# A causal convolution with matrix taps: the first four outputs as direct products, then 21 blocks of twelve

## The chip, the cores and the metric

The kernel runs on one core of a Trainium2 chip. The metric is device time in microseconds (us) of one execution, from one launch; lower is better. The kernel before has three timed runs, with a median of 758.33 us. A core's engines are named as in the profile: PE is TensorE (matmul), DVE VectorE, ACT ScalarE, POOL GpSimd, SP SyncE, which here only issues transfers.

## The reference, cut to what matters

```python
# x: (8, 4096, 512) f32, kernel: (8, 512, 512) f32
out = zeros_like(x)
for k in range(8):
    shifted = x moved by k rows along S, zeros in front
    out += matmul(shifted, kernel[k])
```

So each output row is the sum of eight products of a 512-vector of x, from 0 to 7 rows back, with a 512x512 matrix ("tap" 0 to 7).

## The kernel before, in words

The 8 x 4096 rows are cut into 128 runs of 256 consecutive rows. Run number is the partition, so "output t" (0 to 255) means row t of all 128 runs at once, and `x[t]` is a 128x512 tile. x is kept transposed in bfloat16, four 128x128 pieces to a tile, in the ring `XR` of 20 places (`place(t)`). A product (`product`, line 116) is one such tile times one 512x512 matrix: four matmuls of 128x128 by 128x512, summed in PSUM.

Eight products for each output would be the direct way. The kernel instead takes twelve outputs, t to t+11, as a block of four nodes, each a four-tap filter that gives four rows. The taps are split in two halves, `H1` (taps 4 to 7) and `H0` (taps 0 to 3); the nodes work with `H1`, `H0`, their difference `MI` (H0 - H1) and their sum `PL` (H0 + H1), each on sums or differences of x, and results are combined to rows. Tap `7 - (4a + 2b + c)` lies in `W[H1 or H0, b, c]`, with b and c each LO, HI; MID stands for a difference of LO and HI. Within a node the same trick is used again: a full node takes 9 products (`a1`, `a0`, `u` on the sums A and Z; `v0`, `v1` on S; four `l` on F), and a leaf node 11 (`a1`, `a0`, `u`, then eight on S, without F, `v` and `d`). H0 is a leaf in every block, so a block has 9 + 9 + 9 + 11 = 38 products.

DVE makes the inputs (`zsum`: Z from XR, then A, S, F), the weight sums (`wsum`, `plus`), the differences within PSUM (`node_d`) and, at the end of a node (`node_e`), combines outputs. ACT seeds PSUM (`node_seed`), copies the quad (`node_a1`, `node_dts`) and copies results out. POOL issues the loads from DRAM (they cast f32 to bf16), and transfers that add one SBUF tile to another (`add_h0`, line 328). SP issues the stores and the transposing transfers from a bf16 copy of x in DRAM into XR. Each of these queues works in the order of the program text.

The first 16 outputs of each run (`HEAD`) are made by six nodes of another form, n0 to n5 (lines 303 to 308): n0 as 16 direct products on summed inputs, n1 to n3 as leaves (`LEAF`), n4 and n5 as full nodes; their results are kept (some in the memory of PL weights, `held`) and combined by `node_y`. In this stage the order of the instructions is written out by hand (lines 331 to 561): loads, PE transposes of the first rows, weight sums as taps arrive, fills (matmuls on zeros, whose results are not used) and the six nodes. Then come 20 blocks, whose order is given by the `SLOT` table; node k runs while node k+1 is seeded and the inputs of k+2 are summed.

Memory that is used twice: early x lies in tiles that later hold weights (`xin`), and early results do too; a weight sum into such a tile waits until the last reader, a store among them, is done. PSUM has four pairs of banks; three go round over the nodes, the fourth holds the quad.

Of the kernel before, what the change touches and what calls it, by code (L numbers as in the profile page):

```python
# [14 lines left out]
def kernel(  # L15
# [210 lines left out]
    def node_y(n, b_, a):  # L226
        y = first[n.t, a, b_]
        tt(y, y, n.p[b_], ADD if a == H1 else SUB)

    def store_first(t, a, b_):  # L230
        store(t + 4 * a + 2 * b_, first[t, a, b_])

    def node_e(n, b_):
        p, t = n.p[b_], n.t + 2 * b_
        if n.k < 4:
            y = wide(held[n.k, b_]) if (n.k, b_) in held else y_tile()
            nc.scalar.copy(out=y, in_=p)
            first[n.t, n.a, b_] = y
        elif n.k < 6:
            node_y(n, b_, H1)  # L240
            node_y(n, b_, H0)
        elif n.a == PL:
# [42 lines left out]
    H, HF = XR[:, 8:16], wide(WP[:, 0:8])  # L285
    XF = XR[:, 0:8]
    xin = {(0, 0): WP[:, 12:16], (0, 4): WP[:, 16:20], (8, 0): W[PL, LO, LO], (8, 4): W[PL, HI, LO]}

    def load_xin(t, h):
        rows(xin[t, h], t + h, 4)  # L290
# [12 lines left out]
    nodes = [  # L303
        Node(0, 0, H1),
        Node(1, 8, H1, (T4[:, 0], [D42[:, 7]] + [T42[:, j] for j in range(4)])),
        Node(2, 0, H0, (D4[:, 4], [D42[:, j] for j in range(3, 8)])),
        Node(3, 8, H0, (D4[:, 4], [D42[:, j] for j in range(3, 8)])),
        Node(4, 0, MI), Node(5, 8, MI)]
    nodes += [Node(6 + 4 * k + i, HEAD + STEP * k, a) for k in range(NB)
              for i, a in enumerate((PL, MI, H1, H0))]  # L310
    n0, n1, n2, n3, n4, n5, n6, n7 = nodes[:8]
    def direct(m, t):
        n = K // 2 - 1 - m
        product(n0.p[t // 2][:, t % 2], D4[:, t - m] if t >= m else E4[:, 4 + t - m],
                W[H1, n >> 1, n & 1], m == 0)
# [16 lines left out]
    nc.vector.memset(zero, 0.0)
    for k in range(6):
        fill(pair(k % 4))
    load_xin(0, 0)
    fill(pair(2))
    make_identity(nc, ident)
    transpose_pe("x0", 2, xin[0, 0], 0, 2)
    load_xin(0, 4)
    rows(H[:, 1:4], RUN - 7, 3)  # L340
    nc.sync.dma_start(out=HF, in_=xr[:, RUN - 4:RUN, :])
    load_w(4)
    nc.scalar.copy(out=H[:, 4:6], in_=HF[:, 0:2])
    load_w(5)
    nc.scalar.copy(out=H[:, 6:8], in_=HF[:, 2:4])
    nc.scalar.copy(out=XF[:, 4:6], in_=bank["x0"])
    transpose_pe("h0", 3, H, 4, 6)
    nc.scalar.copy(out=to(XF[:, 0:2]), in_=prev(bank["h0"]))
    first_run(XF[:, 0:2])
    fill(pair(3))  # L350
    fill(pair(2))
    tt(D4[:, 0:2], XF[:, 0:2], XF[:, 4:6], ADD)
    transpose_pe("h1", 0, H, 6, 8)
    nc.scalar.copy(out=to(XF[:, 2:4]), in_=prev(bank["h1"]))
    first_run(XF[:, 2:4])
    fill(pair(3))
    fill(pair(3))
    load_xin(8, 0)
    transpose_pe("xb", 0, xin[0, 0], 2, 4)
    direct(0, 0)  # L360
    load_w(6)
    nc.vector.tensor_copy(out=XF[:, 6:8], in_=bank["xb"])
    tt(D4[:, 2:4], XF[:, 2:4], XF[:, 6:8], ADD)
    direct(0, 1)
    transpose_pe("he", 1, H, 1, 4)
    fill(pair(2))
    fill(pair(2))
    seed_plus(HI, HI)
    direct(0, 2)
    transpose_pe("x1", 2, xin[0, 4], 0, 4)  # L370
    tt(to(E4[:, 1:4]), prev(bank["he"]), to(XF[:, 1:4]), ADD)
    first_run(E4[:, 1:4])
    load_w(7)
    fill(pair(3))
    fill(pair(3))
    direct(1, 1)
    nc.vector.tensor_copy(out=X4, in_=bank["x1"])
    fill(pair(3))
    tt(D42[:, 3], D4[:, 1], D4[:, 3], ADD)
    transpose_pe("x2", 2, xin[8, 0], 0, 4)  # L380
    direct(1, 2)
    load_w(3)
    nc.scalar.copy(out=X8[:, 2:4], in_=bank["x2"][:, 2:4])
    tt(D4[:, 4:8], XF[:, 4:8], X4, ADD)
    tt(D42[:, 4:8], D4[:, 2:6], D4[:, 4:8], ADD)
    wsum(H1, MID, HI)
    wsum(H1, MID, LO)
    direct(2, 0)
    nc.scalar.copy(out=X8[:, 0:2], in_=bank["x2"][:, 0:2])
    tt(T4, X4, X8, ADD)  # L390
    direct(0, 3)
    direct(3, 1)
    nc.scalar.mul(out=W[MI, HI, LO], in_=W[H1, HI, LO], mul=-1.0)
    fill(pair(3))
    direct(3, 0)
    direct(3, 2)
    direct(2, 1)
    wsum(H1, MID, MID)
    tt(AX[1][:, 0], D4[:, 7], T4[:, 0], ADD)
    fill(pair(2))  # L400
    tt(T42[:, 2:4], T4[:, 0:2], T4[:, 2:4], ADD)
    direct(3, 3)
    load_w(1)
    wsum(H0, MID, LO)
    load_w(0)
    load_w(2)
    tt(AX[1][:, 1], T4[:, 0], T4[:, 1], ADD)
    wsum(MI, HI, HI)
    node_a1(n1)
    tt(T42[:, 0:2], D4[:, 6:8], T4[:, 0:2], ADD)  # L410
    direct(2, 2)
    direct(1, 3)
    node_a0(n1)
    node_u(n1)
    node_seed(n1, 0)
    direct(2, 3)
    direct(1, 0)
    wsum(H0, MID, HI)
    wsum(H0, MID, MID)
    load_xin(8, 4)  # L420
    load_x(16)
    node_l(n1, 0, LO)
    tt(AX[0], D4[:, 3:5], D4[:, 4:6], ADD)
    node_e(n0, 0)
    node_seed(n1, 1)
    node_l(n1, 0, HI)
    node_s(n5)
    wsum(MI, LO, HI)
    wsum(MI, MID, HI)
    nc.scalar.copy(out=D4[:, 2:4], in_=T4[:, 2:4])  # L430
    add_h0(MI, HI, LO)
    node_s(n4)
    node_l(n1, 1, HI)
    node_a1(n2)
    wsum(MI, LO, LO)
    node_e(n0, 1)
    node_a0(n2)
    node_e(n1, 0)
    transpose(12, xin[8, 4])
    wsum(MI, LO, MID)  # L440
    tt(D4[:, 4:8], X8, XR[:, 16:20], ADD)
    node_u(n2)
    node_seed(n2, 0)
    seed_plus(LO, HI)
    node_A(n4)
    node_l(n1, 1, LO)
    node_l(n2, 0, LO)
    nc.scalar.copy(out=D42[:, 3], in_=T42[:, 3])
    add_h0(PL, LO, HI)
    node_l(n2, 0, HI)  # L450
    node_seed(n2, 1)
    node_a1(n3)
    node_l(n2, 1, LO)
    tt(AX[1], D4[:, 3:5], D4[:, 4:6], ADD)
    node_u(n3)
    node_a0(n3)
    wsum(MI, MID, LO)
    behind(AX[1][:, 0])
    load_x(36)
    node_e(n1, 1)  # L460
    node_l(n2, 1, HI)
    node_e(n2, 0)
# [174 lines left out]
```

## Time and profile before

| | |
|---|---|
| runs | 757.30, 758.33, 759.14 us; median 758.33 |
| profiled execution | 759.11 us, with a span of 757.3 us from first to last instruction |
| PE busy | 733.1 us, 97% |
| DVE busy | 690.1 us, 91% |
| ACT, POOL busy | 254.9 us, 62.0 us |
| granted PE clock, mean | 0.993 of full |
| DMA | 141.51 MB, mean 187 GB/s |
| weight loads | 8 of 512 KB (as written), median 20.8 us from issue to landing |
| adding transfers, SBUF to SBUF | 5, median 6.8 us |
| stores | 124 of 512 KB from output tiles, median 7.7 us |

Of the page, the slices give the busy share of 40 equal parts of the span in tenths; the answer by stretches gives busy time and instruction count of each engine; the chain follows what ended last back from step to step. A matmul's duration overlaps the next one's, so a rate is read from starts. Line numbers are those of the kernel before.

### The profile page before, as it was taken

How to read it: one execution, taken by the hardware profiler on the slowest of the kernel's cores; microseconds unless marked ns; L12 is line 12 of the kernel's file. 1: busy time of each engine (PE TensorE's matmuls, PEld its weight loads, DVE VectorE, ACT ScalarE, POOL GpSimd, SP SyncE). 2: the span in 40 equal slices, each digit the busy share in tenths (PEclk: the TensorE clock that was granted, in tenths of full speed). 3: DMA queues.
4: the chain of work that ended last, by engine and by line, in shares of the span. 5: the costliest groups of instructions: out<-in, count | busy, mean ns of one | idle time of the engine just before them, and what ended most of it. 6: DMA issues, size and time to landing. Idle time of an engine off the chain costs nothing.

```text
span 757.3 us, 8900 instructions
## 1 busy us (share of the span) xinstructions
PE 733.1 (97%) x3352; PEld 331.8 (44%) x3420; DVE 690.1 (91%) x727; ACT 254.9 (34%) x380; POOL 62.0 (8%) x103
## 2 busy tenths in 40 slices
PE   6999689999999999999999999999999999999997
PEld 2544234444444444444444444444444444444443
DVE  1774899999999999999999999999999999999996
ACT  4264332333333233333323333332423323232331
POOL 5020201010010101101010110101011010100000
PEclk9999899999999999999999999999999999999999
DMA  9979797976959688796968869796786969775424
GB/s 206 207 140 162 195 255 173 211 200 161 245 136 237 162 195 215 149 238 148 243 160 180 241 140 236 146 238 168 185 234 136 242 145 224 184 178 169 136 84 167
DMA packets 159948, 141.51 MB, mean 187 GB/s; under 512 B 130208, under 2 KB 134304, under 8 KB 159776
## 3 DMA queue, kind: packets, MB, share of 16 engines
q1 hardware_dynamic: 145456, 99.89, 48.6%
q0 software_dynamic: 14304, 40.77, 29.6%
q8 instruction: 27, 0.44, 0.2%
q10 hardware_dynamic: 144, 0.26, 0.1%
q14 instruction: 17, 0.14, 0.1%
HBM read 77.33 MB, written 98.57 MB: 232 GB/s over the span
## 4 chain that ended last, share of the span: by engine, by line
PE 91%; DMA 4%; DVE 2%; issue 1%; ACT 0%; POOL 0%; DVEq 0%; ACTq 0%; POOLq 0%
PE pp L118 91%; DMA w<-in_kernel_dram 2%; DMA out_dram<-w 1%; DMA XR<-xd 1%; DVE y L82 1%; DVE w L82 1%; PE pp L295 0%; DVE S L82 0%; PE pp L300 0%; ACT pp L188 0%; DVE Z L82 0%; DVE F L82 0%; ACT pp L169 0%; ACT pp L190 0%; DVE pp L82 0%
## 5 line engine op out<-in xcount | busy, mean ns | idle before, releaser
L118 PE MATMUL pp<-w,S 128*128 128x512 bf16 x1114 | 261.6, 381 | 5.7 <-ACT pp L190 3.9
L118 PE MATMUL pp<-w,F 128*128 128x512 bf16 x973 | 245.3, 379 | 2.9 <-DVE pp L82 1.7
L118 PE MATMUL pp<-w,A 128*128 128x512 bf16 x668 | 173.2, 380 | 3.1 <-ACT pp L169 0.7
L118 PEld LDWEIGHTS <-S 128*128 128x128 bf16 x1136 | 111.2, 98 | 140.7 <-issue 9.5
L82 DVE TENSOR_TENSOR Z<-XR 128x3584 bf16<-128x3584 bf16 (+2 forms) x104 | 146.9, 1430 | 4.1 <-DMA XR<-xd 4.1
L118 PEld LDWEIGHTS <-F 128*128 128x128 bf16 x992 | 97.0, 98 | 119.5 <-issue 2.3
L82 DVE TENSOR_TENSOR S<-Z 128x2560 bf16<-128x2560 bf16 x80 | 118.4, 1480 | 0.0
L188 ACT COPY pp<-pp 128x1024 f32<-128x1024 f32 (+1 forms) x85 | 58.7, 691 | 157.5 <-PE pp L118 152.7
L118 PEld LDWEIGHTS <-A 128*128 128x128 bf16 x680 | 66.2, 98 | 85.7 <-issue 5.2
L172 ACT COPY pp<-pp 128x512 f32<-128x512 f32 x62 | 35.3, 570 | 201.2 <-PE pp L118 201.2
L118 PE MATMUL pp<-w,Z 128*128 128x512 bf16 x378 | 96.8, 379 | 1.0 <-DVE w L82 0.5
L82 DVE TENSOR_TENSOR F<-S 128x1024 bf16<-128x1024 bf16 x124 | 84.5, 682 | 0.0
L107 POOL COPY junk<-A 128x2 bf16<-128x2 bf16 x19 | 18.6, 978 | 540.3 <-DVE A L82 540.3
L190 ACT ACTIVATE pp<-pp 128x1024 f32<-128x1024 f32 (+1 forms) x85 | 59.6, 701 | 4.8 <-DVE y L82 3.8
L118 PEld LDWEIGHTS <-Z 128*128 128x128 bf16 x388 | 38.0, 98 | 46.4 <-issue 0.8
L207 DVE SCALAR_TENSOR_TENSOR pp<-pp,DT 128x512 f32<-128x512 f32 x62 | 42.9, 692 | 16.3 <-PE pp L118 15.6
L247 DVE SCALAR_TENSOR_TENSOR y<-pp,y 128x1024 f32<-128x1024 f32 x40 | 48.8, 1220 | 8.6 <-PE pp L118 8.1
L82 DVE TENSOR_TENSOR A<-Z 128x1024 bf16<-128x1024 bf16 x80 | 54.9, 686 | 1.3
L82 DVE TENSOR_TENSOR y<-y,pp 128x1024 f32<-128x1024 f32 (+1 forms) x46 | 54.3, 1187 | 1.9 <-PE pp L118 1.9
L244 ACT ACTIVATE y<-pp 128x1024 f32<-128x1024 f32 x40 | 41.1, 1027 | 42.2 <-PE pp L118 42.2
L82 DVE TENSOR_TENSOR y<-pp,y 128x1024 f32<-128x1024 f32 x40 | 48.6, 1216 | 1.7 <-DMA out_dram<-y 1.7
L262 DVE SCALAR_TENSOR_TENSOR y<-y 128x1024 f32<-128x1024 f32 x40 | 48.6, 1216 | 0.0
(53 smaller groups left out, 278.8 us busy)
## 6 DMA issues: line engine op xcount, KB each, us to landing
out_dram<-y SPq DMA_DIRECT2D x124, 512.0 KB, 7.7
xd<-in_x_dram POOLq DMA_DIRECT2D x60, 512.0 KB, 10.8
w<-in_kernel_dram POOLq DMA_DIRECT2D x8, 512.0 KB, 20.8
w<-w POOLq DMA_DIRECT2D x5, 512.0 KB, 6.8
w<-in_x_dram POOLq DMA_DIRECT2D x4, 512.0 KB, 11.7
out_dram<-w SPq DMA_DIRECT2D x3, 512.0 KB, 6.8
w<-in_x_dram SPq DMA_DIRECT2D x1, 1024.0 KB, 4.9
XR<-xd SPq DMA_TRANSPOSE x60, 5.4
```

The costliest lines, as they stand in the source:

```text
L82: nc.vector.tensor_tensor(out=o, in0=a, in1=b, op=op)
L107: nc.gpsimd.tensor_copy(out=junk, in_=z[:, 0:2])
L118: nc.tensor.matmul(bank, lhsT=comp[:, c * P:(c + 1) * P], rhs=w[:, c, :], start=start and c == 0, stop=c == DC - 1, skip_group_check=True)
L172: nc.scalar.copy(out=n.q[:, 0], in_=n.q[:, 1])
L188: nc.scalar.copy(out=o, in_=q)
L190: nc.scalar.mul(out=o, in_=q, mul=-1.0)
L207: nc.vector.scalar_tensor_tensor(out=p[:, 0], in0=p[:, 1], scalar=-1.0, in1=DT, op0=MUL, op1=SUB)
L244: nc.scalar.mul(out=cc[b_], in_=p, mul=0.5)
L247: nc.vector.scalar_tensor_tensor(out=dd[b_], in0=p, scalar=-0.5, in1=cc[b_], op0=MUL, op1=ADD)
L262: nc.vector.scalar_tensor_tensor(out=cc[b_], in0=cc[b_], scalar=2.0, in1=dd[b_], op0=MUL, op1=SUB)
```

## The change

The first 16 outputs are no longer a stage of their own. `HEAD` is 4: outputs 0 to 3 are made by 32 direct products, one for each output and tap, as the taps arrive (order 0, 4, 6, 7, 5, 3, 2, 1). Then follow 21 blocks of twelve, the first at output 4. In that block the node order is H1, PL, MI, H0, where the others have PL, MI, H1, H0, and its MI node is a leaf of 11 products (`LEAF = (3,)`). H1's results wait in the memory of two MI weights until `dd` is there (`early_out`). The four corner weights of MI (b and c not MID) are made by ACT, which writes the negated H1 weight, and by an adding transfer on POOL's queue, which adds H0; before, DVE made three of them, and the fourth was made that way, as were the four corners of PL. DVE now makes PL's corners. The first rows of x are loaded in another order and by other queues, and the order of everything before the second block is written anew. Nodes 1 to 4 are the first block; in `go(k, name)`, `name` is a step as in `SLOT` at node k, which may act on node k, k+1 or k+2; steps that a leaf doesn't have do nothing. The loop over the later blocks is the same.

```diff
-LEAF = (1, 2, 3)
+LEAF = (3,)
...
-    HEAD, STEP, R = 2 * K, 12, 20
+    HEAD, STEP, R = K // 2, 12, 20
...
-    D4, D42, zero = WP[:, 0:8], Z[:, 0:8], Z[:, 10]
-    E4, T4, T42 = W[MI, MID, HI], W[MI, MID, LO], W[MI, MID, MID]
-    held = {(2, 1): WP[:, 8:12], (0, 0): WP[:, 12:16], (0, 1): WP[:, 16:20]}
+    H, zero = WP[:, 0:8], DT.bitcast(bf)[:, 0:D]
+    xin = {0: W[MI, MID, MID], 4: W[MI, MID, HI], 8: W[MI, MID, LO]}
...
-        def __init__(self, k, t, a, comps=None):
-            self.k, self.t, self.a, self.comps = k, t, a, comps
-            self.z, self.o = (XR, place(t - 3)) if k < 6 else (Z, 4 if a in (MI, H0) else 0)
-            self.leaf = k in LEAF or k >= 6 and a == H0
+        def __init__(self, k, t, a):
+            self.k, self.t, self.a = k, t, a
+            self.z, self.o = Z, 4 if a in (MI, H0) else 0
+            self.leaf = k in LEAF or a == H0
...
-        else:
+        elif n.k > 4:
             zsum(7, t, t + 8, 4, SUB)
+        else:
+            zsum(4, t - 3, t + 5, 7, SUB)
...
+        elif n.k == 1:
+            early[b_] = wide(W[MI, b_, MID])
+            nc.scalar.copy(out=early[b_], in_=p)
...
+    def early_out(b_):
+        tt(early[b_], early[b_], dd[b_], ADD)
+        store(HEAD + 2 * b_, early[b_])
...
+    def history(eng, t, name):
+        z = XR[:, place(t):place(t) + bank[name].shape[1]]
+        eng(out=to(z), in_=prev(bank[name]))
         nc.vector.memset(z[:, :, 0:D:G], 0.0)
...
+    def here(eng, t, name, a, b):
+        eng(out=XR[:, place(t) + a:place(t) + b], in_=bank[name][:, a:b])
...
+    def load_xin(t):
+        rows(xin[t], t, 4)
...
+    def direct(tap, t):
+        n = K - 1 - tap
+        product(pd[t // 2][:, t % 2], XR[:, place(t - tap)], W[n >> 2, n >> 1 & 1, n & 1], tap == 0)
+    def direct_out(b_):
+        y = y_tile()
+        nc.scalar.copy(out=y, in_=pd[b_])
+        store(2 * b_, y)
     def seed_plus(b_, c_):
         nc.scalar.copy(out=W[PL, b_, c_], in_=W[H1, b_, c_])
 
+    def seed_minus(b_, c_):
+        nc.scalar.mul(out=W[MI, b_, c_], in_=W[H1, b_, c_], mul=-1.0)
...
-    start_n0()
...
+    nodes = [None] + [Node(1 + 4 * k + i, HEAD + STEP * k, a) for k in range(NB)
+                      for i, a in enumerate((PL, MI, H1, H0) if k else (H1, PL, MI, H0))]
...
+    def go(k, name):
+        there, act = step(k)[name]
+        if there:
+            act()
+
+    pd = {0: pair(0), 1: pair(1)}
+    nc.vector.memset(zero, 0.0)
+    go(4, "F1")
+    nc.sync.dma_start(out=XF, in_=xr[:, 0:4, :])
+    for k in range(7):
+        fill(pair(2 + k % 2))
+    cast(nc.scalar.copy, 0, 2)
+    make_identity(nc, ident)
+    rows(H[:, 1:4], RUN - 7, 3)
+    fill(pair(3))
+    rows(H[:, 4:8], RUN - 4, 4)
+    cast(nc.vector.tensor_copy, 2, 4)
+    transpose_pe("x0", 2, xin[0], 0, 4)
+    fill(pair(3))
+    here(nc.scalar.copy, 0, "x0", 0, 2)
+    here(nc.scalar.copy, 0, "x0", 2, 4)
+    fill(pair(2))
+    transpose_pe("h4", 3, H, 4, 8)
+    fill(pair(2))
+    transpose_pe("h3", 2, H, 1, 4)
+    load_w(0)
+    load_xin(8)
+    go(2, "F0")
+    direct(0, 0)
+    history(nc.scalar.copy, -4, "h4")
+    direct(0, 3)
+    history(nc.scalar.copy, -7, "h3")
+    transpose_pe("x8", 2, xin[8], 0, 4)
+    here(nc.scalar.copy, 8, "x8", 0, 2)
+    load_xin(4)
+    here(nc.scalar.copy, 8, "x8", 2, 4)
+    direct(0, 2)
+    transpose_pe("x4", 3, xin[4], 0, 4)
+    here(nc.scalar.copy, 4, "x4", 0, 2)
+    here(nc.scalar.copy, 4, "x4", 2, 4)
+    load_w(4)
+    direct(0, 1)
+    node_z(nodes[1])
+    load_w(6)
+    fill(pair(3))
+    go(2, "dt")
+    load_w(7)
+    direct(4, 2)
+    load_w(5)
+    node_s(nodes[1])
+    direct(4, 0)
+    load_w(3)
+    seed_minus(HI, HI)
+    direct(4, 1)
+    direct(4, 3)
+    go(1, "F1")
+    direct(6, 1)
+    load_w(2)
+    node_A(nodes[1])
+    go(3, "F0")
+    wsum(H1, MID, HI)
+    node_F(nodes[1], 0)
+    wsum(H1, LO, MID)
+    seed_minus(LO, HI)
+    plus((HI, HI))
+    direct(6, 2)
+    wsum(H1, MID, LO)
+    load_w(1)
+    node_a1(nodes[1])
+    direct(7, 2)
+    direct(6, 0)
+    wsum(H1, HI, MID)
+    direct(7, 0)
+    plus((LO, LO))
+    plus((LO, HI))
+    wsum(PL, LO, MID)
+    direct(7, 1)
+    go(2, "d0")
+    direct(6, 3)
+    direct(5, 2)
+    plus((HI, LO))
+    load_x(12)
+    wsum(PL, MID, LO)
+    add_h0(MI, HI, HI)
+    direct(7, 3)
+    node_a0(nodes[1])
+    seed_minus(LO, LO)
+    direct(3, 1)
+    direct(5, 0)
+    wsum(H1, MID, MID)
+    direct(3, 3)
+    direct(5, 1)
+    wsum(PL, MID, HI)
+    direct(3, 2)
+    direct(2, 0)
+    direct(3, 0)
+    go(3, "d0")
+    direct(1, 0)
+    direct(1, 1)
+    node_u(nodes[1])
+    fill(pair(2))
+    direct(5, 3)
+    wsum(H0, MID, LO)
+    direct(2, 1)
+    direct(1, 3)
+    node_dts(nodes[1])
+    wsum(PL, MID, MID)
+    direct_out(0)
+    node_seed(nodes[1], 1)
+    add_h0(MI, LO, HI)
+    node_z(nodes[2])
+    direct(2, 3)
+    node_seed(nodes[1], 0)
+    go(2, "d1")
+    node_v(nodes[1], 1)
+    node_v(nodes[1], 0)
+    node_A(nodes[2])
+    node_d(nodes[1], 1)
+    go(3, "dt")
+    direct(1, 2)
+    wsum(PL, HI, MID)
+    node_d(nodes[1], 0)
+    node_a1(nodes[2])
+    go(3, "v1")
+    go(1, "s")
+    add_h0(MI, LO, LO)
+    go(1, "l10")
+    transpose_x(12)
+    go(1, "l01")
+    go(1, "l00")
+    wsum(H0, MID, HI)
+    go(1, "a0")
+    go(2, "v0")
+    load_x(16)
+    go(1, "u")
+    seed_minus(HI, LO)
+    add_h0(MI, HI, LO)
+    go(1, "F0")
+    direct(2, 2)
+    direct_out(1)
+    go(1, "z")
+    go(2, "v1")
+    go(1, "A")
+    wsum(MI, MID, HI)
+    go(1, "s0")
+    transpose_x(16)
+    go(1, "l11")
+    go(1, "e0")
+    go(1, "v0")
+    wsum(MI, MID, LO)
+    go(1, "s1")
+    wsum(MI, MID, MID)
+    go(3, "v0")
+    go(1, "dt")
+    go(1, "e1")
+    go(1, "v1")
+    go(1, "d0")
+    go(2, "F1")
+    go(1, "a1")
+    go(2, "l00")
+    go(2, "u")
+    go(2, "a0")
+    go(2, "l01")
+    load_x(20)
+    go(2, "s0")
+    go(2, "s")
+    go(3, "l01")
+    go(3, "l00")
+    go(1, "d1")
+    go(2, "l11")
+    load_x(24)
+    go(3, "F1")
+    go(2, "l10")
+    go(2, "z")
+    go(3, "s")
+    go(3, "d1")
+    go(2, "e0")
+    go(2, "s1")
+    go(2, "e1")
+    go(2, "A")
+    go(3, "e0")
+    go(3, "l11")
+    wsum(H0, MID, MID)
+    go(3, "l10")
+    load_x(28)
+    go(2, "a1")
+    go(3, "a0")
+    go(3, "u")
+    transpose_x(20)
+    go(3, "s0")
+    early_out(0)
+    load_x(32)
+    go(4, "l00")
+    go(3, "e1")
+    wsum(MI, LO, MID)
+    middle(nodes[3], 1)
+    early_out(1)
+    middle(nodes[3], 0)
+    go(3, "z")
+    go(3, "s1")
+    go(4, "l01")
+    go(4, "l11")
+    go(3, "A")
+    go(4, "b1")
+    go(4, "l10")
+    transpose_x(24)
+    load_x(36)
+    go(3, "r")
+    go(4, "u")
+    go(4, "e0")
+    go(4, "s")
+    go(4, "a0")
+    go(4, "s0")
+    go(4, "v0")
+    wsum(MI, HI, MID)
+    go(4, "s1")
+    go(4, "dt")
+    go(4, "z")
+    go(4, "A")
+    go(4, "v1")
+    go(4, "d0")
+    go(4, "F0")
+    go(4, "d1")
+    go(4, "e1")
+    go(4, "a1")
+    for k in range(5, len(nodes)):
+        for name in SLOT[nodes[k].a].split():
+            go(k, name)
```

More of the change, by code (lines that the diff above doesn't have):

```diff
@@ L45 @@
     ypool = ctx.enter_context(tc.tile_pool(name="y", bufs=5))
-    dpool = ctx.enter_context(tc.tile_pool(name="xd", bufs=NB * STEP // 4, space=bass.MemoryType.DRAM))
+    dpool = ctx.enter_context(tc.tile_pool(name="xd", bufs=RUN // 4 - 3, space=bass.MemoryType.DRAM))
     ppool = ctx.enter_context(tc.tile_pool(name="p", bufs=1, space=PSUM))
@@ L144, in node_z @@
             zsum(0, t - 7, t + 1, 7, SUB)
+        elif n.k > 4:
+            zsum(7, t, t + 8, 4, SUB)
         else:
-            zsum(7, t, t + 8, 4, SUB)
+            zsum(4, t - 3, t + 5, 7, SUB)
     def node_A(n):
@@ L160, in comps @@
         s, a = SX[n.k % 2], AX[n.k % 2]
-        u, s = n.comps or (n.z[:, n.o + 3], [s[:, j] for j in range(5)])
-        return u, [a[:, 0], a[:, 1]], s, [F[:, j] for j in range(4)]
+        return (n.z[:, n.o + 3], [a[:, 0], a[:, 1]], [s[:, j] for j in range(5)],
+                [F[:, j] for j in range(4)])
     def node_a1(n):
@@ L219, in store @@
         nc.sync.dma_start(out=orr[:, t:t + 2, :], in_=y)
-    first, cc, dd = {}, {}, {}
+    cc, dd, early = {}, {}, {}
     def y_tile():
         return ypool.tile([P, 2, D], f32, name="y")
[L226 to L231, printed above, removed]
     def node_e(n, b_):
         p, t = n.p[b_], n.t + 2 * b_
[L235 to L242, printed above, removed]
+        if n.a == PL:
             cc[b_] = y_tile()
@@ L283, in plus @@
             tt(W[PL, b_, c_], W[H0, b_, c_], W[H1, b_, c_], ADD)
[L285 to L290, printed above, removed]
     bank = {}
@@ L302, in transpose_pe @@
         bank[name] = o[:, 0:t1 - t0]
[L303 to L315, printed above, removed]
     def to(z):
@@ L319, in prev @@
         return z.rearrange("p t (c m) -> p t c m", m=P)[:, :, :, 0:P - 1]
-    def first_run(z):
+    def history(eng, t, name):
+        z = XR[:, place(t):place(t) + bank[name].shape[1]]
+        eng(out=to(z), in_=prev(bank[name]))
         nc.vector.memset(z[:, :, 0:D:G], 0.0)
-    X4, X8 = XR[:, 8:12], XR[:, 12:16]
-    def start_n0():
-        n0.p = {0: pair(0), 1: pair(1)}
+    def here(eng, t, name, a, b):
+        eng(out=XR[:, place(t) + a:place(t) + b], in_=bank[name][:, a:b])
+    def load_xin(t):
+        rows(xin[t], t, 4)
@@ L325, in seed_plus, with cast @@
+    XF = wide(WP[:, 8:16])
+    def cast(eng, a, b):
+        eng(out=xin[0][:, a:b], in_=XF[:, a:b])
+    def direct(tap, t):
[5 more added lines that the diff above has]
+        store(2 * b_, y)
     def seed_plus(b_, c_):
         nc.scalar.copy(out=W[PL, b_, c_], in_=W[H1, b_, c_])
+    def seed_minus(b_, c_):
+        nc.scalar.mul(out=W[MI, b_, c_], in_=W[H1, b_, c_], mul=-1.0)
@@ L328, in add_h0 @@
     def add_h0(a, b_, c_):
         nc.gpsimd.dma_start(out=W[a, b_, c_], in_=W[H0, b_, c_], accum_op=ADD)
-    start_n0()
[L332 to L462, printed above, removed]
-    node_seed(n3, 1)
-    node_seed(n3, 0)
-    wsum(MI, MID, MID)
-    node_a1(n4)
-    transpose_x(16)
-    tt(D42[:, 4:8], D4[:, 2:6], D4[:, 4:8], ADD)
-    node_l(n3, 0, LO)
-    node_F(n4, 1)
-    node_l(n3, 0, HI)
-    plus((MID, LO))
-    node_e(n2, 1)
-    plus((MID, HI))
-    node_e(n3, 0)
-    load_x(20)
-    node_a0(n4)
-    node_u(n4)
-    node_l(n3, 1, LO)
-    node_seed(n4, 0)
-    wsum(MI, HI, MID)
@@ L482 @@
-    node_seed(n4, 1)
-    node_dts(n4)
-    node_v(n4, 1)
-    node_F(n4, 0)
-    node_v(n4, 0)
-    node_A(n5)
-    transpose_x(20)
-    node_d(n4, 1)
-    node_l(n3, 1, HI)
-    node_d(n4, 0)
-    node_z(n6)
-    node_s(n6)
-    node_l(n4, 0, HI)
-    node_l(n4, 0, LO)
-    node_a1(n5)
-    node_l(n4, 1, HI)
-    node_y(n4, 0, H1)
-    load_x(44)
-    node_A(n6)
-    node_a0(n5)
-    node_y(n4, 0, H0)
-    node_l(n4, 1, LO)
-    load_x(48)
-    node_y(n4, 1, H0)
-    node_F(n5, 0)
-    node_z(n7)
@@ L508 @@
-    store_first(0, H1, 0)
-    seed_plus(LO, LO)
-    add_h0(PL, HI, HI)
-    node_dts(n5)
-    node_y(n4, 1, H1)
-    node_u(n5)
-    store_first(0, H0, 0)
-    node_e(n3, 1)
-    node_seed(n5, 1)
-    node_v(n5, 1)
-    node_F(n5, 1)
-    node_seed(n5, 0)
-    node_v(n5, 0)
-    node_a1(n6)
-    node_a0(n6)
-    node_d(n5, 1)
-    behind(AX[0][:, 0])
-    node_d(n5, 0)
-    add_h0(PL, LO, LO)
-    load_x(40)
-    node_A(n7)
-    node_l(n5, 0, HI)
-    wsum(PL, LO, MID)
-    store_first(0, H0, 1)
@@ L532 @@
-    plus((MID, MID))
-    seed_plus(HI, LO)
-    node_l(n5, 0, LO)
-    node_y(n5, 0, H0)
-    node_l(n5, 1, LO)
-    node_y(n5, 0, H1)
-    add_h0(PL, HI, LO)
-    node_l(n5, 1, HI)
-    node_u(n6)
-    load_x(24)
-    store_first(0, H1, 1)
-    load_x(28)
-    node_F(n6, 0)
-    node_seed(n6, 0)
-    node_v(n6, 0)
-    store_first(8, H1, 0)
-    node_seed(n6, 1)
-    store_first(8, H0, 0)
-    wsum(PL, HI, MID)
-    node_dts(n6)
-    node_y(n5, 1, H0)
-    load_x(32)
-    node_y(n5, 1, H1)
-    node_d(n6, 0)
@@ L556 @@
-    node_a1(n7)
-    store_first(8, H1, 1)
-    node_v(n6, 1)
-    transpose_x(24)
-    store_first(8, H0, 1)
-    node_d(n6, 1)
-    later = {6: ((H1, LO, MID),), 7: ((H1, HI, MID),)}
+    nodes = [None] + [Node(1 + 4 * k + i, HEAD + STEP * k, a) for k in range(NB)
+                      for i, a in enumerate((PL, MI, H1, H0) if k else (H1, PL, MI, H0))]
     SLOT = {
@@ L568, with step @@
     }
-    for k in range(6, len(nodes)):
+    def step(k):
         cur = nodes[k]
@@ L600 @@
         }
-        for abc in later.get(k, ()):
-            wsum(*abc)
-        for name in SLOT[cur.a].split():
-            there, act = acts[name]
-            if there:
-                act()
+        return acts
+    def go(k, name):
[8 more added lines that the diff above has]
+        fill(pair(2 + k % 2))
```

## The prediction

> **What bounds the kernel now.** I read the busy row and the slices of the page first, then the answer by stretches, then the PE's timeline and the chain for the stretch in which PE is not full.
>
> ```profile
> span 757.3 us, 8900 instructions
> ...
> PE 733.1 (97%) x3352; PEld 331.8 (44%) x3420; DVE 690.1 (91%) x727; ACT 254.9 (34%) x380; POOL 62.0 (8%) x103
> ...
> PE   6999689999999999999999999999999999999997
> ...
> DVE  1774899999999999999999999999999999999996
> ```
>
> PE is full from slice 7 on; what can be won lies in slices 0 to 5 (a slice is 18.9 us). DVE is nearly full too, so work that DVE gets late is not caught up quickly. By stretches (columns: stretch, length, then busy time and count of each engine, granted clock, DMA share, GB/s):
>
> ```profile
> 70.00:80.00 10.00, 7.49 (x34) 3.32 (x34) 5.90 (x7) 3.79 (x4) 0.00 (x0) 1.00 0.37 63
> 80.00:90.00 10.00, 7.52 (x23) 2.82 (x23) 9.45 (x11) 3.44 (x4) 1.79 (x4) 0.66 0.98 247
> 90.00:100.00 10.00, 6.47 (x28) 2.62 (x28) 8.54 (x9) 2.23 (x4) 2.28 (x4) 1.00 1.04 238
> 100.00:110.00 10.00, 9.83 (x46) 4.32 (x46) 10.00 (x11) 4.03 (x6) 0.00 (x0) 1.00 1.05 303
> 103.43:136.36 32.93, 32.77 (x149) 14.81 (x153) 32.86 (x34) 10.52 (x18) 2.52 (x4) 1.00 0.88 215
> 136.36:169.29 32.93, 32.77 (x151) 14.86 (x152) 31.72 (x33) 10.87 (x18) 2.52 (x4) 1.00 0.81 193
> ```
>
> A full PE does 46 matmuls in 10 us; the three stretches from 70 to 100 do 85 instead of 138. DVE needs 31.7 of a block's 32.9 us. The chain there (start, length, what):
>
> ```profile
> 66.35 8.99 DMA XR<-xd
> 75.43 1.24 DVE Z L82
> 76.69 1.49 DVE S L82
> ...
> 82.20 9.21 DMA out_dram<-w
> 91.44 1.23 DVE w L82
> ...
> 102.77 0.61 DVE F L82
> 103.39 0.05 issue
> 103.43 7.73 PE pp L118 x35
> ```
>
> x of 20 to 23 is transposed late because its place in XR is still in use; then a DVE backlog, then DVE behind the store of an early output held in PL's weight memory. From 103.43 on the chain is PE alone. That instant is the product `l11` of the PL node of the block at output 16; from there on both kernels issue the same 20 blocks. So the question is when the changed kernel starts that product.
>
> **What the Trainium skill says.** *TensorE: Matmul & The Clock Gate*, "What's actually happening": the array runs at half clock after an idle window of about 3.4 us. The trace agrees: PE idles 3.86 us before 81.77, and then 8 matmuls take 3.57 us (0.43 each, not 0.216); PEclk is 0.66. The same page, "Architectural detail", says that ACT and DVE are strict first-in first-out: a DVE operation that waits holds up all behind it, as at 91.44. *DMA: Bandwidth & Descriptors*, "Anatomy of one DMA — SWDGE", gives 2.0 us plus bytes by 436 GB/s, 3.2 us for 512 KB alone; here it is 5.1 to 6.8 us for an adding transfer that finds the queue nearly empty, 12.1 and 16.6 behind others, and 2.5 us from one landing to the next in a full queue. Measurements are used.
>
> **The change, part by part.** A product is four matmuls; 16 of them start from 60.97 to 64.43, so one takes 0.866 us.
>
> *Products.* Removed: 16 direct ones on summed inputs, three leaf nodes of 11, two nodes of 9: 67. Added: 32 direct, and a block of H1 9, PL 9, MI 11, H0 11 (MI of the first block is made a leaf): 72. That is +5 products, +4.3 us. Transposes stay 76; fills go from 36 to 26 matmuls.
>
> *DVE.* Weight sums 21 before, 22 after, at 1.13 us from start to start (bf16 2048 elements; 1.22 long): +1.1 us. The four corners of MI go to ACT (1.92 us each, the row of the negating copy) and POOL's queue. A 3584 sum is 1.94 us pitch, 2560 1.40, 1024 0.60, a PSUM operation of 1024 1.13.
>
> *Loading.* In the trace the POOL transfers land at 8.2, 10.6, 12.4 (384 KB), 15.5 (tap 4), 18.0, 20.4, 23.0 ... 29.1, 31.7, 34.3, 36.8, 39.3: 2.5 us each. Tap 4 is behind 1.9 MB there. Now in front of it are 384 KB and four of 512 KB, so it lands two units later, at 20.5; tap 0 at 13, x of 8 to 11 at 15.4, of 4 to 7 at 17.8. After it: tap 6 at 23, 7 at 26, 5 at 28.6, 3 at 31, 2 at 33.6, 1 at 36.2. make_identity now precedes POOL's first load (about 0.6 us); the 1 MB of SP, landed at 5.6, covers it; uncovered it costs 0.6.
>
> *PE up to tap 4.* Four products of tap 0, 32 transposes and one fill fit between 13 and 20.5 even at half clock (6.9 us of products when cold). From 20.5 on, 78 products and a fill stand ahead of `l11` of PL: 78 x 0.866 + 0.4 = 68.0, so 88.5 without a wait. The waits, walking each engine's list in order:
>
> 1. ACT places the last x at about 21; DVE then does Z, S, F, A (1.94 + 1.40 + 0.60 + 0.60), and H1's (MID,HI) at 26.7. PE wants it for `a1` of H1 at 25.7: **1.0**.
> 2. Direct products cover DVE's weight sums: (MID,LO) of H1 at 30.6 for 33.7, (MID,MID) at 39.6 for 42.3, PL's (MID,MID) at 43 for 54. Each tap is landed when its products come. No wait.
> 3. DVE stands from 45.6 to 48.1 for `d1` of H1. It loses 2.5 us there, which come back in step 5.
> 4. After the last direct product (55.8) ACT must copy the outputs out (1.02), seed (0.58), copy H1's result (1.02), seed again; PE has one product per gap: 1.6 - 0.87, twice, with 0.2 of matmul tail each: **1.8**.
> 5. The fourth MI corner: ACT negates after its copy for `a1` of PL, 51.2 to 53.1; POOL's adding transfer takes 5.1 to 6.8, so about 59. DVE reaches MI's (MID,LO) at 57.3, waits 1.7, ends (MID,MID) at 61.3; PE comes at 59.9: **1.3**. The other three are issued by 36 and landed by 50.
> 6. MI and H0 are leaves: their seeds are 1024 wide (1.0 us) and the quad needs ACT's negated copy (0.58): **0.5** before `l01` of MI, **0.7** and **1.3** at `a0` and `l00` of H0.
> 7. DVE: MI's `e1` at 76.4, then MI's (LO,MID), whose memory holds the first early output. That store goes out at 73.1; DMA is then quiet (x up to 39 is loaded; the next loads wait for the A after it), so I take 3.5 us (the trace has 2.6 to 10.6 for such stores): 76.6, no loss. Then middles, early output, Z, A, `e0`, S, (HI,MID), Z, A, `d0`, F0, `d1`, `e1`, S, F1: F1 ends at 96.0. PE, with the waits so far (6.6) at 95.1, waits **1.0**.
>
> Sum 7.6: `l11` at 96.1 against 103.43, so 7.3 us earlier. x of 20 to 23 may be transposed from 66.4 (H0's Z has read the place) and takes 9.0 as before: 75.4, wanted at 81.4; if that cover of 6 is gone, each further us costs one. x of 12 is wanted at 64.5 and is on SP since 47. Store of the second early output: 80.2, wanted at 86.6. Nothing else changes: the tail of 4.4 us after the last product stays.
>
> Profiled span: 757.3 - 7.3 = **750.0**. The runs shown have a median of 758.33, 1.0 above the span; carried over, **751.0**.
>
> Bounds of what the trace doesn't show: all waits vanish but those of steps 1 and 4, 746 (a gain beyond that is excluded, since tap 4 cannot land before the data ahead of it); stores and the adding transfer at the longest of the trace, below.
>
> **Rivals.**
>
> *A. The early store takes the place of the old one.* For: the chain has 9.21 us for the same kind of store, and in the loop stores take 7.7. Against: at 73 no load is running by my list. At 9 us it lands at 82, DVE waits 5.5 at (LO,MID), PE idles at `a1` of the next PL: 751.0 + 5 = 756.
>
> *B. Slower: the fourth corner is late.* Its adding transfer lies in POOL's queue, and the trace has one that took 16.6 us behind x loads. It then lands at 70, DVE stops for 11 at MI's (MID,LO), PE idles about 9.5, and the clock is halved after it (2 to 3 us): 751.0 + 12 = 763. It decides from a landing at about 68 on (9 us later than I take). Against: x of 16 is issued at 36 and landed by 52, x of 20 is issued behind it.
>
> *C. Loading gives the gain back.* All of PE and DVE hang on taps 4 and 6. The array waits for weights until 20.5 rather than 15.6; if tap 4 came at 27 (slower transfers while DVE works), the end is 757.5, no change. Against: the pitch of 2.5 us holds from 8 to 41 us.
>
> **How the numbers follow.** Forecast (747 to 754.5) 0.62, A 0.15, C 0.08, B 0.15. Two in a thousand, 1.5 us, is about what a measurement can tell. Faster: 0.62 + 0.15 = 0.77; same 0.08; slower 0.15. The range goes from the bound of 746 over A to the edge of C, 758, and leaves out B and little else.
>
> **What would show it.** Right: `l11` of the second PL at 94 to 98, PE full after it; no PE gap over 3 us after 20, so PEclk stays near 1.0; 5 products more in all. Tap 4 at 20 to 21; a chain in which no DMA stands after 60 except 1 to 2 us at MI's weights. Wrong: DVE standing at a weight sum for a store or an adding transfer for over 4 us, tap 4 after 23, or a PEclk of 0.6 to 0.7 between 55 and 100.

## The result: 1 us faster, where 7 were forecast

In the first comparison the changed kernel took 756.27 us (median of 4 runs, 755.81 to 757.71), the kernel before 757.82 (756.68 to 759.14): ratio 0.9982, 95% interval 0.9960 to 1.0004. A second, closer comparison gave 756.54 (22 runs) against 757.53 (48 runs): 0.9985, interval 0.9975 to 0.9995. So the change gains 0.15%, about 1.1 us, less than the 1.5 us that the prediction called no difference. The forecast of 751.0 is missed by 5.3 us; the measured time lies inside the range of 746 to 758.

The page of the changed kernel:

```profile
span 754.3 us, 8893 instructions
...
PE 732.9 (97%) x3362; PEld 331.7 (44%) x3430; DVE 691.1 (92%) x719; ACT 250.7 (33%) x374; POOL 60.8 (8%) x101
...
PE   7998899999999999999999999999999999999997
...
DVE  0887799999999999999999999999999999999996
```

PE is again full except in the first slices and the last. The deep hole of before (slice 4) is gone; two slices of 8 stand in its place. The same kernel by stretches (stretch, length, busy time and count of PE, PE loads, DVE, ACT and POOL, granted clock, DMA share, GB/s):

```profile
50.00:60.00 10.00, 8.59 (x39) 3.81 (x39) 8.19 (x8) 5.86 (x7) 3.49 (x6) 1.00 0.78 120
60.00:70.00 10.00, 7.81 (x29) 2.92 (x27) 9.68 (x9) 3.58 (x6) 0.00 (x0) 0.83 1.06 234
70.00:80.00 10.00, 9.22 (x43) 4.14 (x43) 4.72 (x4) 2.60 (x3) 0.00 (x0) 1.00 1.08 220
80.00:90.00 10.00, 7.75 (x36) 3.27 (x35) 8.51 (x9) 1.93 (x2) 1.06 (x3) 1.00 0.52 172
```

Two stretches are short of matmuls: 60 to 70 (29, where a full PE does 46, at a clock of 0.83) and 80 to 90 (36). The chain of what ended last names both causes:

```profile
53.75 0.28 issue
54.03 6.01 DMA w<-w
60.05 0.02 issue
60.07 1.24 DVE w L81
...
62.62 5.33 PE pp L117 x16
...
76.82 4.55 DMA out_dram<-w
...
81.46 1.23 DVE w L81
```

`w<-w` is the adding transfer of MI's fourth corner, `out_dram<-w` the store of the first early output. Both keep DVE waiting at a weight sum, as the store alone did before. `l11` of the PL node at output 16, the point from which both kernels issue the same work, starts at 100.24 (103.43 before, 96.1 forecast). That is 3.2 us earlier, and the profiled spans differ by 3.0.

### The profile page after: what moved, and what is told of

It reads as the page before. It is cut to its first block, busy times and chain, and to the rows that moved or that the text cites. A ratio compares the mean times of both kernels' runs of the same rounds, so it can differ in the third digit from the quotient of the medians.

```text
span 754.3 us, 8893 instructions
## 1 busy us (share of the span) xinstructions
PE 732.9 (97%) x3362; PEld 331.7 (44%) x3430; DVE 691.1 (92%) x719; ACT 250.7 (33%) x374; POOL 60.8 (8%) x101
## 4 chain that ended last, share of the span: by engine, by line
PE 91%; DMA 4%; DVE 2%; issue 1%; ACT 1%; POOL 0%; DVEq 0%; SPq 0%; ACTq 0%; POOLq 0%
PE pp L117 91%; DMA w<-in_kernel_dram 2%; DMA w<-w 1%; DVE w L81 1%; DMA out_dram<-w 1%; DVE Z L81 1%; DVE y L252 0%; POOL w L87 0%; ACT pp L189 0%; ACT w L328 0%; DVE y L81 0%; ACT pp L173 0%; DVE A L81 0%; DVE S L81 0%; DVE pp L81 0%
## 5 line engine op out<-in xcount | busy, mean ns | idle before, releaser
L117 PE MATMUL pp<-w,S 128*128 128x512 bf16 x1174 | 274.1, 379 | 4.8 <-ACT pp L189 2.9
L117 PEld LDWEIGHTS <-S 128*128 128x128 bf16 x1200 | 117.1, 98 | 147.1 <-issue 8.1
L81 DVE TENSOR_TENSOR Z<-XR 128x3584 bf16<-128x3584 bf16 (+2 forms) x108 | 155.2, 1456 | 6.0 <-ACT XR L305 6.0
L81 DVE TENSOR_TENSOR S<-Z 128x2560 bf16<-128x2560 bf16 x84 | 124.7, 1485 | 0.1
L189 ACT COPY pp<-pp 128x512 f32<-128x512 f32 (+1 forms) x84 | 57.8, 688 | 157.3 <-PE pp L117 154.5
L117 PE MATMUL pp<-w,Z 128*128 128x512 bf16 x330 | 86.0, 381 | 2.3 <-DVE w L81 1.9
L81 DVE TENSOR_TENSOR A<-Z 128x1024 bf16<-128x1024 bf16 x84 | 57.9, 690 | 1.5
L191 ACT ACTIVATE pp<-pp 128x512 f32<-128x512 f32 (+1 forms) x84 | 58.7, 698 | 0.1
L81 DVE TENSOR_TENSOR y<-y,pp 128x1024 f32<-128x1024 f32 (+1 forms) x43 | 51.1, 1190 | 1.9 <-PE pp L117 1.9
L117 PEld LDWEIGHTS <-Z 128*128 128x128 bf16 x336 | 32.9, 98 | 41.9 <-DVE w L81 2.4
```

Of the source, the lines that this page charges most:

```text
L81: nc.vector.tensor_tensor(out=o, in0=a, in1=b, op=op)
L117: nc.tensor.matmul(bank, lhsT=comp[:, c * P:(c + 1) * P], rhs=w[:, c, :], start=start and c == 0, stop=c == DC - 1, skip_group_check=True)
L189: nc.scalar.copy(out=o, in_=q)
L191: nc.scalar.mul(out=o, in_=q, mul=-1.0)
```

## The experiments

Every edit is made on the changed kernel; the last one is made on top of the edits of "Both edits". Ratios are to the kernel before, measured in the same comparison. Behind an edit, line numbers shift by its own lines.

### Both kernels once more

> The changed kernel once more, for a closer ratio. The product l11 of the second PL node starts at 100.2 in its trace against 103.4 in the profiled execution of before, but that execution (759.1) was 1.3 above before's median. Theory: the true gain is what the medians say, 1.5 us, ratio 0.998, because before's first 100 us vary from run to run with its DMA waits. Rival: the gain is the 3.0 us of the two spans, ratio 0.996.

Measured: ratio 0.9985 as above, so the medians are right and the spans of the first two profiles overstate the gain. The kernel before spreads over 754.7 to 760.0 us, the changed one over 755.5 to 758.4, and the spread of the former goes with the granted clock that is listed for each execution. Of its 48 executions, 26 were granted a mean clock of 0.993 or less and took 758.9 us in the mean; 17 were granted 0.996 or more and took 755.8. Of the 22 of the changed kernel none is below 0.994, and its 17 at 0.996 or more took 756.4. So the gain of 1.1 us lies against the executions of the kernel before that lose clock; set against those that keep it, the changed kernel is not faster. Whether the lower clock makes those executions longer, or both follow from longer waits, is not shown.

> The kernel before, profiled once more. Theory (its profiled execution was a slow one, held up by the store of 9.2 us at 82 to 91): l11 of the PL node at output 16 starts 1 to 2 us earlier than 103.4, with a shorter wait for a store. Rival (the difference lies elsewhere, in the loading or in the loop): l11 again at 103 to 103.8.

Measured: a span of 755.7 (757.44 us), `l11` at 101.76. The chain of this second profile of the kernel before:

```profile
64.96 8.34 DMA XR<-xd
73.40 1.24 DVE Z L82
...
80.18 9.68 DMA out_dram<-w
...
101.76 3.41 PE pp L118 x15
```

My theory of where it varies fell: the store took longer (9.68, not 9.21). 1.4 of the 1.7 us were there at the start of the chain already. The PE timelines show where it comes from. First the profiled execution of before:

```profile
12.10 1.24 PE L295 MATMUL pp<-Z 128*128 128x512 bf16 x4
...
15.61 0.56 PE L118 MATMUL pp<-w,w 128*128 128x512 bf16 x1 [1.64 <-DMA w<-in_kernel_dram]
16.38 2.77 PE L118 MATMUL pp<-w,w 128*128 128x512 bf16 x6 [0.22 <-issue]
```

and the same in its second profile:

```profile
12.97 1.71 PE L295 MATMUL pp<-Z 128*128 128x512 bf16 x4
...
15.91 1.89 PE L118 MATMUL pp<-w,w 128*128 128x512 bf16 x8 [0.78 <-DVE XR L362]
```

The same eight matmuls (L118; one record is missing in the first) ran at half clock in one execution, 0.43 us each, and at full clock in the other. The second execution was not spared the half clock: it fell earlier there, on fills (L295) and transposes, after which the first product started only 0.3 us later. Its granted clock was 0.66 from 10 to 15 us and 1.00 from 15 to 20; in the first execution it was 1.00 and then 0.66. So what varied is where the half clock fell, ahead of the first products or on them. The forecast set its 7.3 us against an execution that was itself about 1.6 us above the median of 757.5.

### The fourth corner earlier

```diff
     seed_minus(LO, LO)
+    seed_minus(HI, LO)
...
     add_h0(MI, LO, LO)
+    add_h0(MI, HI, LO)
...
     go(1, "u")
-    seed_minus(HI, LO)
-    add_h0(MI, HI, LO)
```

> The fourth corner of MI is negated by ACT at about 31 us, where ACT stands idle, and its adding transfer is issued behind the third corner's. Theory (corner wait and the half clock after it cost 2.5 to 3.4 us): DVE doesn't wait at MI's (MID,LO), a1 of MI starts near 61 in place of 62.6, the clock stays full in 60 to 70, the end is 2.5 to 3.4 us earlier than the changed kernel. Rival (the store of the first early output limits anyway): the end moves by less than 1 us.

Measured: 753.61 us, ratio 0.9952 (0.9933 to 0.9971), 2.9 us faster than the changed kernel in the same comparison; its slowest run (754.70) is faster than the fastest of the changed kernel (755.53). In the changed kernel DVE waits for the corner and PE for DVE; the line of DVE, then the PE timeline:

```profile
60.07 2.48 DVE L81 TENSOR_TENSOR w<-w,w 128x2048 bf16<-128x2048 bf16 x2 [1.70 <-DMA w<-w]
```

```profile
59.68 1.02 PE L117 MATMUL pp<-w,S 128*128 128x512 bf16 x4 [0.52 <-ACT pp L191]
62.62 1.60 PE L117 MATMUL pp<-w,Z 128*128 128x512 bf16 x4 [1.91 <-DVE w L81]
64.01 1.91 PE L117 MATMUL pp<-w,F 128*128 128x512 bf16 x4
65.71 2.22 PE L117 MATMUL pp<-w,A 128*128 128x512 bf16 x8
67.77 1.03 PE L117 MATMUL pp<-w,F 128*128 128x512 bf16 x4
```

and with the corner early:

```profile
60.66 1.02 PE L117 MATMUL pp<-w,S 128*128 128x512 bf16 x4 [0.52 <-ACT pp L191]
61.80 1.04 PE L117 MATMUL pp<-w,Z 128*128 128x512 bf16 x4
62.68 1.03 PE L117 MATMUL pp<-w,F 128*128 128x512 bf16 x4
63.57 1.89 PE L117 MATMUL pp<-w,A 128*128 128x512 bf16 x8
65.29 1.03 PE L117 MATMUL pp<-w,F 128*128 128x512 bf16 x4
```

The first PE line is `v1` of PL, the second `a1` of MI, the last `l01` of PL. From first to last it takes 8.09 us in the one and 4.63 in the other. About half of the 3.5 us is the wait; the rest is slow matmuls: `a1` and the next product take 1.39 and 1.70 from start to start, where 0.87 is normal. The theory holds, for the wait and the half clock behind it taken together. The edit has a new wait of its own. POOL now issues five x loads at 38 to 45 us, which in the changed kernel stand behind the fourth corner, at 54.6 and later, and the transposing transfer of x 12 to 15 takes 20.0 us from issue to landing (6.1 in the changed kernel). That it shares the DMA with these loads is the likely reason, not a tested one. DVE waits 3.58 us for it, where in the changed kernel it stood 2.97 us for PE a little later.

### MI's (LO,MID) later

```diff
     go(3, "e1")
-    wsum(MI, LO, MID)
...
+    wsum(MI, LO, MID)
     wsum(MI, HI, MID)
```

> MI's (LO,MID), which waits for the store of the first early output, is summed later, beside (HI,MID). Theory: DVE's 2.3 us of waiting are gone, a1 of the second PL doesn't wait (1.1 us), the end is 1.1 to 1.5 us earlier than the changed kernel, since PE is then next. Rival (this wait only fills time that DVE would have spent waiting for PE): no difference, under 0.4 us. The half clock at 62 to 67 stays in both.

Measured: 754.60 us, ratio 0.9966 (0.9955 to 0.9978), 1.9 us faster than the changed kernel. There the weight sum waits for the store, and `a1` of the next PL for DVE:

```profile
81.46 1.23 DVE L81 TENSOR_TENSOR w<-w,w 128x2048 bf16<-128x2048 bf16 x1 [2.28 <-DMA out_dram<-w]
...
88.88 1.04 PE L117 MATMUL pp<-w,A 128*128 128x512 bf16 x4 [1.06 <-DVE A L81]
```

With the sum late DVE has no wait there, and `a1` follows its predecessor without a gap:

```profile
89.07 1.03 PE L117 MATMUL pp<-w,A 128*128 128x512 bf16 x4
```

Its profiled execution (756.29) was above its median, so the gain is read from the medians. The distance between `a1` of H1 and `l11` in the profiles is 71.85 us, against 73.05 and 72.16 in the two of the changed kernel. That is 1.2 and 0.3 us less; where the rest of the 1.9 comes from, the profiles do not show.

### Both edits

> Both edits: the fourth corner early, and MI's (LO,MID) late. Theory: the gains add, 3.5 to 4.7 us earlier than the changed kernel, near the 750 us span of the prediction. Rival (the two waits stand in for one another): no more than the better of the two alone, 2.5 to 3.4.

Measured: 752.73 us, ratio 0.9942 (0.9921 to 0.9963), 3.8 us faster than the changed kernel, span 750.7. The PE timeline at the common point:

```profile
95.57 1.03 PE L117 MATMUL pp<-w,Z 128*128 128x512 bf16 x4
96.59 1.04 PE L117 MATMUL pp<-w,F 128*128 128x512 bf16 x4
```

`l11` (the second line) at 96.59, where the forecast had 96.1. Two gains of 2.9 and 1.9 give 3.8; with an interval of 1.6 us to either side this cannot be told from a full sum. The theory holds. This is the fastest version of the study.

### The half clock alone

```diff
     go(2, "F1")
+    for _ in range(4):
+        warm = pair(3)
+        for h in range(2):
+            nc.tensor.matmul(warm[:, h], lhsT=XR[:, 9, 0:P], rhs=XR[:, 9], start=True, stop=True)
     go(1, "a1")
```

> Eight matmuls whose results are overwritten stand ahead of a1 of MI, so that PE works while it would wait for the fourth corner; the waits themselves stay. Theory (the half clock after that gap costs by itself): the granted clock of 60 to 70 is full, l01 of MI starts about 1.5 us earlier after a1 of MI than in the changed kernel, and the end is 1.0 to 1.7 us earlier. Rival (a slow PE there is hidden by DVE, which is late anyway): under 0.4 us.

Measured: 755.98 us, ratio 0.9985 (0.9976 to 0.9994), the same as without the fill. The granted clock is full in 60 to 70, and PE's timeline has no slow matmul:

```profile
60.61 2.54 PE L537 MATMUL pp<-XR 128*128 128x512 bf16 x8
63.20 1.02 PE L117 MATMUL pp<-w,Z 128*128 128x512 bf16 x4
64.06 1.03 PE L117 MATMUL pp<-w,F 128*128 128x512 bf16 x4
```

PE is 1.1 us ahead at `a1` of H0 (76.61, not 77.70), and DVE gives it back:

```profile
76.86 1.22 DVE L234 SCALAR_TENSOR_TENSOR y<-pp,y 128x1024 f32<-128x1024 f32 x1 [1.67 <-issue]
80.71 1.23 DVE L81 TENSOR_TENSOR w<-w,w 128x2048 bf16<-128x2048 bf16 x1 [2.62 <-DMA out_dram<-w]
```

The store lands at 80.7 instead of 81.4, and DVE waits 2.62 us, not 2.28; PE then stands 1.40 at the next `a1`. The rival was right for this kernel: in the profile the half clock is hidden by the store. I took SP's queue for the reason that the store didn't come earlier, since the transposing transfers of x 16 and 20 hold SP from 58.0 to 77.4, and tested it.

```diff
-    early_out(0)
     load_x(32)
+    load_x(36)
+    early_out(0)
...
-        store(HEAD + 2 * b_, early[b_])
+        eng = nc.gpsimd if b_ == 0 else nc.sync
+        eng.dma_start(out=orr[:, HEAD + 2 * b_:HEAD + 2 * b_ + 2, :], in_=early[b_])
```

> The fill ahead of a1 of MI, and the store of the first early output issued by POOL, so that it isn't behind the transposing transfers of x 16 and 20 on SP (their issue held SP from 58 to 77). MI's (LO,MID) stays where it was. Theory (SP's queue makes that store late): it is issued near 75.3 rather than 77.4, DVE waits under 1.5 us rather than 2.6 at (LO,MID), the end is 0.7 to 1.6 us earlier than with the fill alone, ratio about 0.997. Rival (the transfer itself is slow while x is transposed): it lands near 80.7 as before, ratio 0.9985.

Measured: 756.13 us, ratio 0.9986 (0.9976 to 0.9997): nothing gained. POOL issued the store at 76.63, 0.3 us after the output was summed, and it took 4.5 us (3.2 with the fill alone); DVE still waited:

```profile
78.01 1.22 DVE L234 SCALAR_TENSOR_TENSOR y<-pp,y 128x1024 f32<-128x1024 f32 x1 [1.68 <-issue]
81.22 1.23 DVE L81 TENSOR_TENSOR w<-w,w 128x2048 bf16<-128x2048 bf16 x1 [1.99 <-DMA out_dram<-w]
```

This execution ran 1.1 us behind the other from `a1` of H1 on. Counted from `a1` of MI the store went out 1.9 us earlier, as the theory had it, but landed only 0.6 earlier; DVE's wait is 0.6 shorter and so is the way to `l11`, which the medians do not show. So SP's queue was not the main cause: the transfer itself takes 2.6 to 4.6 us in the profiles that have this wait, and there is only one DVE operation to spend it on.

> The fill ahead of a1 of MI, and MI's (LO,MID) summed late. Theory (the half clock costs PE 1.1 us, which the store of the first early output hid in the run with the fill alone, because that store left SP at 77 either way): 1.0 us earlier than with the late sum alone, ratio to before about 0.995. Rival (the half clock is hidden by something else too): the same as with the late sum alone, 0.9966.

With the fill and the late sum together: 754.88 us, ratio 0.9968 (0.9956 to 0.9979), as with the late sum alone (0.9966). In the profiles `l11` comes 70.66 us after `a1` of H1, against 71.85 without the fill, so the half clock cost 1.2 us in that execution; the medians do not show it, so the theory failed, and that the store hid the half clock before is not confirmed. Each interval is 0.9 us to either side, so what the half clock costs on average stays open: between nothing and about 1 us. It need not strike in every run: five of the 22 executions of the changed kernel were granted a clock of 1.0, and they took 756.2 us in the mean, the others 756.7.

### The corners on DVE

The four `seed_minus` and `add_h0` calls are taken out, and DVE makes the corners:

```diff
+    wsum(MI, HI, HI)
+    wsum(MI, LO, HI)
     wsum(MI, MID, HI)
...
+    wsum(MI, LO, LO)
+    wsum(MI, HI, LO)
     wsum(MI, MID, LO)
```

> One part of the change undone: DVE makes the four corners of MI, just ahead of MI's (MID,HI) and (MID,LO); the negating copies and the adding transfers are gone. Theory (DVE is the scarce engine here): DVE has 4.5 us more to do and 1.7 us less to wait, so a1 of MI is 2.8 us later, and with the longer gap of PE the end is 3 to 5 us later than the changed kernel. Rival (the adding transfers cost as much as they save): the end moves by less than 1 us either way.

Measured: 758.81 us, ratio 1.0017 (1.0006 to 1.0027), 0.3%, or 2.4 us, slower than the changed kernel, a bit less than expected. PE's timeline:

```profile
59.94 1.02 PE L117 MATMUL pp<-w,S 128*128 128x512 bf16 x4 [0.52 <-ACT pp L191]
65.87 1.89 PE L117 MATMUL pp<-w,Z 128*128 128x512 bf16 x4 [4.91 <-DVE w L81]
67.55 1.91 PE L117 MATMUL pp<-w,F 128*128 128x512 bf16 x4
```

PE waits 4.91 us instead of 1.91, and the next dozen matmuls are slow. So giving the corners to ACT and DMA pays, also with the late fourth one; without that part the change is 0.17% slower than the kernel before.

### More work for PE while ACT seeds

On top of both edits: `a1`, `a0` and `u` of H0 ahead of `l10` of MI, the next block's Z and A ahead of MI's `e1`, and the five x loads held until A of MI.

```diff
+    behind(AX[1][:, 0])
     load_x(20)
...
+    wsum(H0, MID, MID)
     go(3, "e0")
+    go(2, "a1")
     go(3, "l11")
-    wsum(H0, MID, MID)
-    go(3, "l10")
     load_x(28)
-    go(2, "a1")
     go(3, "a0")
...
     go(3, "s0")
+    go(3, "l10")
     early_out(0)
+    go(3, "z")
+    go(3, "A")
...
-    go(3, "z")
...
-    go(3, "A")
```

> Both edits of before, the next x loads held behind A of MI (so that they don't slow the transposing transfer of x 12), and l10 of MI put after u of H0, with the next Z and A ahead of MI's e1, so that PE works while ACT seeds H0. Theory (the gaps of 0.73 and 1.14 us at H0 are ACT's latency and can be covered): 1.5 to 2.2 us earlier than both edits alone, a span near 749. Rival (DVE's order then makes the next a1 late): no gain or a loss up to 1 us.

Measured: 762.48 us, ratio 1.0070 (1.0055 to 1.0086), 9.8 us slower than both edits alone. PE has no gap from 68 to 88, as meant, and then a hole:

```profile
100.02 1.89 PE L117 MATMUL pp<-w,A 128*128 128x512 bf16 x4 [8.27 <-DVE A L81]
```

Two waits of DVE make it:

```profile
80.35 1.23 DVE L81 TENSOR_TENSOR Z<-XR 128x2048 bf16<-128x2048 bf16 x1 [6.14 <-DMA XR<-xd]
...
96.00 1.23 DVE L81 TENSOR_TENSOR w<-w,w 128x2048 bf16<-128x2048 bf16 x1 [5.07 <-DMA out_dram<-w]
```

The three parts were not run apart, so the share of each is open. The early Z asks for x of 20 to 23 before it is transposed and stands 6.14 us with all of DVE's queue behind it; the second early output is stored late (85.93) and lands while the next loads are running. Theory and rival both missed it: the rival had DVE late, but by 1 us.

## Why the prediction was wrong, step by step

**The point of comparison.** The gain was rightly read as the shift of one instant, `l11` at output 16, in front of identical work. But 103.43 belonged to an execution that was about 1.6 us above the median (half clock at its first direct products), which makes the gain of 7.3 too large, not the time of 751.0. And 1.0 us was carried over from span to device time: it mixed the span of one execution with the median of others. In one and the same execution the two differ by 1.8 for the profiled kernel before and by 2.0 to 2.1 in the first four runs of the changed one. That is 1.0 us of the miss of 5.3; the span made up the rest, 754.3 against 750.0.

How the miss of 4.1 us at `l11` builds up in the profile of the changed kernel:

| instant | forecast | measured | late by |
|---|---|---|---|
| `a1` of H1 | 26.7 | 27.19 | 0.5 |
| `v1` of PL | 59.0 | 59.68 | 0.7 |
| `a1` of MI | 61.3 | 62.62 | 1.3 |
| `l01` of PL | 64.8 | 67.77 | 3.0 |
| `l11` at output 16 | 96.1 | 100.24 | 4.1 |

The forecast of `v1` is one product before "PE comes at 59.9", that of `l01` four products of 0.866 after `a1`.

**The count of products, the loading and the start.** Five products more is in the program's order; the trace lacks some records, so it can't be counted there. Tap 4 landed at 21.8, not 20.5, 17.3 us after its issue. (In the kernel before it stood behind 1.4 MB; the 1.9 MB of the prediction count its own 512 KB. The two units added are right.) PE began 1.3 late, but the wait of step 1 shrank from 1.0 to nearly none, so 0.5 us of the miss is left. Ten profiles of the changed kernel and its edits have this start between 21.6 and 23.1, so 20.5 was too early in all. Rival C had the right place and a fifth of its size, 1.3 of 6.5 us.

**Steps 2 to 4** held. The last direct product started at 55.41 and so ended at 56.3 (55.8 forecast); `v0` and `v1` of PL cost 1.7 us more from start to start than two products, where 1.8 was forecast.

**Step 5 is the first that failed.** DVE's wait was right to the tenth, 1.70 us, with the transfer at 6.01 and landed at 60.04 (59 forecast). But PE's wait was 1.91, not 1.3, and step 5 stopped there: after it the array ran at half clock to about 67, which the prediction put at nothing. It had excluded that because no single gap was over 3 us; none was, and the half clock came all the same. From `v1` to `l01` of PL the trace has 8.09 us, the forecast 5.8: 0.7 of the difference is the longer wait, 1.7 are slow matmuls. Taking the late corner away, and with it both, gave 2.9 us at the end. How much of that is the half clock stays open: with the fill alone the end did not move.

**Step 7 is the second.** MI's `e1` ended at 79.2 for 76.4, 2.8 late from the causes above. The store of the first early output went out at 76.82 for 73.1, 3.7 late (0.5 of it on SP's queue), and took 4.55 us, not 3.5. DVE waited 2.28 us at (LO,MID), which the prediction calls "no loss", and PE 1.06 at the next `a1`. This is rival A's wait at less than half its price: the store landed at 81.4, near rival A's 82, but because it left late, not because it took 9 us. That rival A's 756 is near the measured time is luck. Taking the wait away gave 1.9 us. Two smaller terms of the same stretch were wrong and offset each other: the wait of 1.0 for F1 before `l11` shrank to 0.2, and PE waited 0.66 at 94.03 for ACT's seed, which the prediction does not have.

**Step 6** held (0.73 and 1.14 at H0 for 0.7 and 1.3, 0.28 for 0.5).

With both causes taken away the span is 750.7 for 750.0 and `l11` comes at 96.59 for 96.1. That is in part luck. PE began 2.1 us late there (22.61), and the edit cut the wait of 1.3 at step 5, which the forecast includes, to 0.3.

Of the signs named beforehand, `l11` lies outside 94 to 98, the granted clock of 0.83 in 60 to 70 lies between right and wrong, and a store of 4.55 us stands in the chain at 77, where none should. Rival B named the right transfer; it was 1 us late, not 9.

The range held the time because rivals A and C kept it wide. The chance of no difference, 0.08, was far too low: the forecast's gain was a sum of waits that were each costed at their single best value, and the large errors all made the kernel slower.

## What to carry to other kernels

When PE's wait is cut to a short one rather than to none, cost the half clock as well as the gap. Here it followed a gap of 1.9 us behind two of 0.84 and 0.52 in all three profiles that have these gaps; with the third gap at 0.3 or filled it did not. Whether the two short ones matter was not tested. A weight sum that waits for a store belongs as late in DVE's order as its reader allows, and a transfer that needs another engine's result first should start when that engine is idle, not where its result is wanted. Take the time of the kernel before from its median, and ask whether the one profiled execution was a usual one.

## What the runs showed that was not expected

Half clock after gaps of 0.84, 0.52 and 1.91 us within 57 to 62.6, none of them near the 3.86 of the kernel before. The half clock of the kernel before's start on its first products in one execution and ahead of them in another, worth 1.4 us. And the issue of one transposing transfer held SP's queue for 13.65 us (57.96 to 71.6, in the changed kernel) with five x loads in the queues, for 15.5 with the corner early, and for 2.9 at 81 to 86 us in five of the runs. What decides between them was not tested.
